# Which side of the on-chip memory the Fourier stage and the late weights lie on

## The chip, the cores and the metric

The kernel runs on one core of one Trainium2 chip, as one program. The metric is device time in microseconds (us) from start to end of the program. The times of the kernel before are 3048.86, 3058.79 and 3046.28 us (median 3048.86). "Within the measurement" below means within 0.5% of that, some 15 us.

## The reference, cut to what matters

The reference is one layer of an encoder over 1024 + 2048 tokens of width 1024, all in float32:

```python
u = rms_norm(h, norm_w)
z_f, u_f, z_s, xbc, dt_raw = split(u @ w_in)
four = fft2(u_f.reshape(b, s, 8, 64), axes=(1, 3), norm='ortho').real
y_f = einsum('bsgc,gcd->bsgd', four, w_fmix) * silu(z_f)
xbc = silu(conv1d_depthwise(xbc, conv_w) + conv_b)
y_s = ssd(xs, dt_f, A_f, B, C) + flip(ssd(flip(xs), ...)) + D * xs
y_s = group_rms_norm(y_s * silu(z_s)) * ssd_norm_w
h = h + concat([y_f, y_s]) @ w_out
h = h + (p @ w_ple_in) * sigmoid(h @ w_ple_gate)
y = rms_norm(h, final_norm_w)
```

## The kernel before, in words

The work has four stages, one after the other, with their edges overlapped.

**Stage 1, projections and SSD** (lines 102 to 821), three blocks of 1024 tokens. The normalized rows, turned and split into a high and a low part, lie in six tiles `uh0` to `uh2` and `ul0` to `ul2` of pool `up` (10,944 bytes in each partition). For each 128 columns of `w_in`, `piece` (line 340) makes 24 matmuls for each third of the tokens (L359). Around these pieces stands the SSD work of 12 units: `decays` loads 128 KB decay rows `er` (L633), `states` makes the states `H` (L605, L616), `diag` and `across` make `y` (L573, L647, L650, L651), `gated` multiplies by the gate on GpSimd (L656), `out` stores `y` (L665). The order of this stage is written out by hand, step by step. After the last piece some steps are left that hold only the end of the last unit: here "the tail". The pools of stage 1, from the left end of the memory to the right: `up` (normalized rows), `wp` (input weights: `wr`, `wh`, `wl`), `t4`, `cp` (conv rows and constants), `gp` and `sp` and `dp` (SSD tiles).

**Stage 2, Fourier** (lines 868 to 1033), eight steps: four of 1024 tokens, then four of 2048. Each loads `U` (L900) and the gate `Z` (L966), folds `U` (`Ue`, `Uo`, `fold0` to `fold3`: L969 to L979, on VectorE and GpSimd), multiplies by a small matrix (`pm` L959, `pq` L1004), splits the product (`qh` L1007, `ql` L1008) and multiplies by tables `th`, `tl` (L1013, `pr`). `yv` is put together on VectorE (L1023 to L1027), multiplied by `Z` on GpSimd (L1031) and stored (L1032). The tables come raw from DRAM into `traw` (L915) and are split (L916, L917). `th0` to `tl1` lie in pool `ft_`, `th2` to `tl3` in `fc`, what a step reads first in `fp`, the rest in `fq`.

**Stage 3, output product** (from line 1138), 24 pairs of 128-row tiles in 2 x 2 block products of Strassen's kind with weights `P1` to `P7`, each in a high tile `whP` and a low tile `wlP`. The raw weight is loaded into the low tile (L845), ScalarE copies it into the high tile (L847), VectorE leaves the rest in the low one (L848). `P1`, `P2`, `P6` lie in pool `wa` and are loaded during stage 2. `P5`, then `P7`, `P4`, `P3` lie in `wb` over tiles of stage 2; the loads of the second pair's `y` (L1158) are queued behind `P5`'s load (`issue_after`). The first pair is in `y_first` (pool `ox`). The other tiles are in `mp` and `yp`.

**Stage 4** is the gated second input and the last norm, with tiles of `mp` and `q4`.

Outside stage 1 a planner orders the instructions: it runs the program on a model of the engines, and each engine gets, when it is free in the model, the earliest instruction of the program that is ready. An instruction that writes a tile is ready once the tiles that held these bytes are done with (`reuse_waits="tile"`). The planner may also put instructions of stage 2 between the ones of stage 1 that were ordered by hand. On the chip each engine, SyncE's DMA queue among them, follows that order strictly.

A pool is placed on the left (the first goes lowest, next ones above) or on the right (the first goes highest, next ones below). Within a pool tiles ascend in the order in which they first appear. So it follows from the sizes what lies over what.

Of the kernel before, what the change touches and what calls it, by code (L numbers as in the profile page):

```python
# [9 lines left out]
F32 = mybir.dt.float32  # L10
# [5 lines left out]
PSUM = bass.MemoryType.PSUM  # L16
DRAM = bass.MemoryType.DRAM

P = 128
# [37 lines left out]
def tile_hybrid_encoder(ctx: ExitStack, tc: tile.TileContext, a):  # L57
# [767 lines left out]

    R_ = dict(side="right", reuse_waits="tile")
    L_ = dict(side="left", reuse_waits="tile")
    ox = ctx.enter_context(tc.tile_pool(name="ox", bufs=1, **L_))
    wa = ctx.enter_context(tc.tile_pool(name="wa", bufs=1, **L_))


    NAMES = ("P1", "P2", "P6", "P5", "P7", "P4", "P3")
# [6 lines left out]
    def product_weights(m, names, W):  # L839

        for name in names:
            pool = wa if name in NAMES[:3] else wb
            wh, wl = first_w.pop(name, None) or weight_tiles(pool, name)
            raw = wl.bitcast(F32)
            ld = nc.sync.dma_start(raw, WSd[m][:, NAMES.index(name)])  # L845
            for k in range(4):
                S.copy(wh[:, k, :], raw[:, k, :])  # L847
                V.tensor_tensor(wl[:, k, :], raw[:, k, :], wh[:, k, :].bitcast(F32), op=ALU.subtract)  # L848
            W[name] = (wh, wl)
        return ld  # L850

    def group_rstd(y, sq, sh, pb, rs):

        S.activation(sq, y.rearrange("p (r k) l -> p r k l", r=2)[:, :, 1:4, :], AF.Square)
        for j in (1, 2):
            G.tensor_tensor(sq[:, :, 0, :], sq[:, :, 0, :], sq[:, :, j, :], op=ALU.add)  # L856
        S.copy(sh[:, 0], sq[:, :, 0, :])
        G.tensor_tensor(sh[:, 1], sq[:, :, 0, :], sh[:, 0].bitcast(F32), op=ALU.subtract)
        for j in range(2):
            T.matmul(pb, lhsT=ones_r, rhs=sh[:, j], start=(j == 0), stop=(j == 1))  # L860
        S.activation(rs, pb, AF.Sqrt, bias=eps4, scale=1.0 / 384.0)
        V.reciprocal(rs, rs)

    def group_scale(y, rs):
        ssd = y.rearrange("p (r k) l -> p r k l", r=2)[:, :, 1:4, :]
        G.tensor_tensor(ssd, ssd, rs.unsqueeze(2).broadcast_to([P, 2, 3, P]), op=ALU.mult)

    with ExitStack() as ph:
        ft_ = ph.enter_context(tc.tile_pool(name="ft_", bufs=1, **R_))
        fp = ph.enter_context(tc.tile_pool(name="fp", bufs=2, **R_))  # L870
        fq = ph.enter_context(tc.tile_pool(name="fq", bufs=2, **L_))
        fc = ph.enter_context(tc.tile_pool(name="fc", bufs=1, **L_))
        fpr = ph.enter_context(tc.tile_pool(name="fpr", bufs=1, space=PSUM, **R_))
        fpl = ph.enter_context(tc.tile_pool(name="fpl", bufs=1, space=PSUM, **L_))
        shapes = dict(yv=([2048], 1, F32), Z=([2048], 1, F32), qh=([4, P], 2, F32R), ql=([4, P], 2, F32R),
                      ee=([512], 1, F32), eo=([512], 1, F32), ed=([2], 2, F32))

# [5 lines left out]
        def fq_next(tag):  # L883
            return fq_first.pop(tag) if tag in fq_first else fq_tile(tag)
# [47 lines left out]
        for step, (seq, f) in enumerate(order):  # L932
# [17 lines left out]
            def table(i, part, k):  # L950

                if N == 2048:
                    return tabs[i][part][:, k, :]
                return tabs[i % 2][part][:, k, i // 2:512:2]

            scale = 0.5 / math.sqrt(N * 64.0)
            pm = fpr.tile([P, 2, P], F32, tag="pm", name="pm")
            for i in range(2):
                T.matmul(pm[:, i, :], lhsT=bd[:, i, :], rhs=wbd[:, f, :], start=True, stop=True)  # L959
            mt = fp.tile([P, 2, P], F32, tag="mt", name="mt")  # L960
# [22 lines left out]
            S.activation(junk[:, 0:H + 1], Ue[:, 0:M + 1:2], AF.Copy, accum_out=edge[:, 1:2])  # L983
            S.activation(junk[:, 0:H], Ue[:, 1:M:2], AF.Copy, accum_out=edge[:, 2:3])
            V.tensor_tensor(edge[:, 1:2], edge[:, 1:2], edge[:, 2:3], op=ALU.subtract)
            pe = fpr.tile([P, 2], F32, tag="pm", name="pe")
            T.matmul(pe, lhsT=mats[0], rhs=edge[:, 0:2], start=True, stop=True)
            ed = fq_next("ed")
            V.tensor_copy(ed, pe)

            if last:
                for q in range(2):
                    pb = fpr.tile([P, 2, P], F32, tag="pm", name="pb")
                    sq = fp.tile([P, 2, 3, P], F32, tag="Uo", bufs=1, name="sq")
                    sh = fp.tile([P, 2, 2, P], F32R, tag="traw", name="sh")
                    rs = fp.tile([P, 2, P], F32, tag="fold0", name="rs")
                    group_rstd(y_first[:, q], sq, sh, pb, rs)
                    group_scale(y_first[:, q], rs)

            res = []  # L1000
            for i in range(4):
                pq = fpr.tile([P, 4, P], F32, tag="pq", bufs=2, name="pq")
                for k in range(kt):
                    T.matmul(pq[:, k, :], lhsT=folds[i][:, k * P:(k + 1) * P], rhs=mats[i % 2], start=True, stop=True)  # L1004
                qh = fq_next("qh")
                ql = fq_next("ql")
                S.copy(qh[:, :kt, :], pq[:, :kt, :])  # L1007
                V.tensor_tensor(ql[:, :kt, :], pq[:, :kt, :], qh[:, :kt, :].bitcast(F32), op=ALU.subtract)  # L1008
                pr = (fpr if i < 2 else fpl).tile([P, 512], F32, tag="pr", bufs=2 + i // 2, name="pr")
                n = 0  # L1010
                for k in range(kt):
                    for qt, part in ((qh, 0), (qh, 1), (ql, 0)):
                        T.matmul(pr[:, :H], lhsT=qt[:, k, :], rhs=table(i, part, k), start=(n == 0), stop=(n == 3 * kt - 1))  # L1013
                        n += 1
                res.append(pr)
# [13 lines left out]
            for q in range(N // TB):  # L1029
# [7 lines left out]

    wb = ctx.enter_context(tc.tile_pool(name="wb", bufs=1, **L_))  # L1040

    placed = {x: wb.tile([P, 4, 512], F32R, tag=f"w{x}", name=f"w{x}")
              for x in ("hP3", "hP4", "lP3", "lP4", "lP7", "lP5", "hP5", "hP7")}
    for name in NAMES[3:]:
        first_w[name] = placed["h" + name], placed["l" + name]
    mp = ctx.enter_context(tc.tile_pool(name="mp", bufs=1, **R_))
    mps = ctx.enter_context(tc.tile_pool(name="mps", bufs=1, space=PSUM, reuse_waits="tile"))
    todo = [(bi, c) for bi in range(3) for c in range(NCH)]
    NP = len(todo) // 2
# [58 lines left out]
    def turned(i):  # L1108

        hts, E = [], []  # L1110
        for bi, c in todo[2 * i:2 * i + 2]:
            hts.append(residual(Hd[bi * NCH + c]))

        def turn(src, nk):
            pt = mps.tile([P, 4, P], F32, tag="sm", bufs=3, name="pt")
            for k in range(nk):
                T.transpose(out=pt[:, k, :], in_=src[:, k * P:(k + 1) * P], identity=ident)
            return pt

        def kept21():  # L1120
            t = mp.tile([P, 4, P], F32, tag="s32", bufs=3, name="s32")
            S.copy(t, turn(hts[1], 4))
            return t
        A = halves(lambda: turn(hts[0], 4), lambda: turn(hts[0][:, 512:], 4), kept21, lambda: turn(hts[1][:, 512:], 4))
        for bi, c in todo[2 * i:2 * i + 2]:
            b = BLOCKS[bi]
            r0 = b["t0"] + c * P
            pl = q4.tile([P, 256], F32, tag="pl", bufs=2, name="pl")
            nc.sync.dma_start(pl, a["p"][b["seq"]][r0:r0 + P, :])
            pt = turn(pl, 2)  # L1130
            eh = q4.tile([P, 2, P], F32R, tag="eh", bufs=2, name="eh")
            el = q4.tile([P, 2, P], F32R, tag="el", bufs=2, name="el")
            S.copy(eh, pt[:, :2, :])
            V.tensor_tensor(el, pt[:, :2, :], eh.bitcast(F32), op=ALU.subtract)
            E.append((eh, el))
        return A, hts, E

    with ExitStack() as ph:
        yp = ph.enter_context(tc.tile_pool(name="yp", bufs=1, **R_))
        hbs, behind = [], []  # L1140

        def incoming(p):
            hb = yp.tile([P, 6, P], F32, tag="hb", name="hb")
            nc.sync.dma_start(hb, HBd[:, 6 * p:6 * p + 6, :])
            hbs.append(hb)
# [84 lines left out]
        for n, (p, i) in enumerate(steps):  # L1230
            cur, after = ready, coming
            with tc.issue_after(ld.ins):
                if n + 2 < len(steps):
                    if steps[n + 2] == (1, 0):
                        incoming(1)
                    coming = prepare(*steps[n + 2])
                if n + 1 < len(steps):
                    ready = after()
                else:
                    ph.close()  # L1240
                    q4 = ctx.enter_context(tc.tile_pool(name="q4", bufs=1, **R_))
                    ready = turned(0)
            outputs(i, W, *cur)
            if i == NP - 1:
                W = {}
                last_w = product_weights(p + 1, NAMES, W)
# [126 lines left out]
```

## Time and profile before

| | |
|---|---|
| median of three runs | 3048.86 us |
| profiled execution, its own time | 3053.19 us |
| its span, first to last instruction | 3051.3 us |
| TensorE busy (share of span) | 2837.5 us (93%) |
| TensorE weight loads | 2568.8 us (84%) |
| VectorE busy | 2238.1 us (73%) |
| ScalarE busy | 1387.5 us (45%) |
| GpSimd busy | 1477.0 us (48%) |
| mean granted TensorE clock | 0.973 |

Stage 1 ends near 1998 us, stage 2 near 2130 us, stage 3 near 2740 us. A busy share is a mean over stages with other limits; what a change of one seam is worth is read at that seam. Clock 1.00 is 2.4 GHz, 0.50 is 1.2 GHz.

### The profile page before, as it was taken

To read this page: it belongs to the slowest core of one execution; us is meant where nothing else is said; L and a number is where in the kernel's file an instruction comes from. 1 tells how busy PE (TensorE), PEld (TensorE's weight loads), DVE (VectorE), ACT (ScalarE), POOL (GpSimd) and SP (SyncE) were. 2 spreads that over 40 slices of the span, in tenths; PEclk is the share of its full clock that TensorE was granted. 3 is DMA by queue.
4 is the path that set the end of the run, shared out by engine and by line. 5 is a ranking of instruction groups with operands and counts; after the bars stand their busy time and mean duration, and the time that the engine had idled before them with its cause. 6 is when DMAs were issued, how large, how long until landed. Compare 5 with 4: busy or idle time off the path is not lost.

```text
span 3051.3 us, 47045 instructions
## 1 busy us (share of the span) xinstructions
PE 2837.5 (93%) x17252; PEld 2568.8 (84%) x17252; DVE 2238.1 (73%) x3412; ACT 1387.5 (45%) x2980; POOL 1477.0 (48%) x1114
## 2 busy tenths in 40 slices
PE   4999999999999989989999999969899989989998
PEld 4999988988999888978999999957677777768887
DVE  3687867766687667667679787677988988866665
ACT  3545455443544455433444444433434433355554
POOL 0355646441467566642555554455677688610000
PEclk9999999999999999999999999979999999999999
DMA  2378978872778678862677787665554644352221
GB/s 89 79 123 160 158 162 169 143 140 81 128 167 168 148 174 170 150 167 69 118 145 157 159 146 155 115 207 209 203 178 138 228 152 153 130 203 90 93 82 71
DMA packets 454579, 440.56 MB, mean 144 GB/s; under 512 B 24384, under 2 KB 405444, under 8 KB 450508
## 3 DMA queue, kind: packets, MB, share of 16 engines
q1 hardware_dynamic: 454060, 436.50, 59.8%
q8 instruction: 137, 2.24, 0.3%
q14 instruction: 94, 0.77, 0.1%
q10 hardware_dynamic: 288, 1.05, 0.1%
HBM read 328.41 MB, written 110.10 MB: 144 GB/s over the span
## 4 chain that ended last, share of the span: by engine, by line
PE 52%; DMA 15%; DVE 13%; POOL 9%; issue 6%; ACT 3%; SPq 2%; POOLq 0%; DVEq 0%; ACTq 0%
PE ps L359 27%; PE X L1089 6%; DMA wr<-in_w_in 4%; PE Z L1089 3%; DMA R<-ROWd 3%; PE pst L605 3%; DMA xt<-in_x_sample 2%; PE po L647 2%; PE W L1279 2%; DVE al L1060 2%; PE pd L573 2%; POOL wl L188 2%; DVE s L1065 2%; PE Y L1089 1%; POOL sq L856 1%
## 5 line engine op out<-in xcount | busy, mean ns | idle before, releaser
L359 PE MATMUL ps<-uh,wh 128*128 128x342 f32 (+1 forms) x2880 | 961.0, 334 | 5.2 <-ACT wh L187 5.2
L359 PE MATMUL ps<-uh,wl 128*128 128x342 f32 (+1 forms) x2880 | 927.7, 322 | 3.7 <-POOL wl L188 3.7
L359 PE MATMUL ps<-ul,wh 128*128 128x342 f32 (+1 forms) x2880 | 925.7, 321 | 0.0
L188 POOL TENSOR_TENSOR wl<-wr,wh 128x1024 fp32r<-128x1024 f32 x120 | 302.8, 2523 | 733.4 <-ACT wh L187 705.0
L359 PEld LDWEIGHTS ps<-uh,wh 128*128 128x128 f32 x2880 | 551.9, 192 | 16.4 <-ACT wh L187 5.7
L359 PEld LDWEIGHTS ps<-ul,wh 128*128 128x128 f32 x2880 | 554.2, 192 | 1.0 <-issue 1.0
L359 PEld LDWEIGHTS ps<-uh,wl 128*128 128x128 f32 x2880 | 550.5, 191 | 4.6 <-POOL wl L188 4.3
L556 ACT ACTIVATE R<-R,lb 128x128 f32<-128x128 f32 x1152 | 355.6, 391 | 69.7 <-POOL R L546 69.6
L546 POOL TENSOR_SCALAR_AFFINE_SELECT R<-R 128x512 f32<-128x512 f32 x288 | 260.3, 915 | 179.0 <-DMA R<-ROWd 168.7
L616 DVE SCALAR_TENSOR_TENSOR H<-H,cd,pst 128x64 f32<-128x64 f32 x888 | 182.7, 275 | 54.9 <-PE pst L605 51.9
L400 DVE SCALAR_TENSOR_TENSOR xT<-raw,cvt,xT 128x1024 f32<-128x1024 f32 x144 | 213.7, 1484 | 2.6
L365 ACT COPY raw<-ps 128x342 f32<-128x342 f32 x180 | 78.4, 439 | 279.2 <-PE ps L359 263.3
L1089 PE MATMUL X<-whP,ah 128*128 128x512 f32 x480 | 195.8, 408 | 8.4 <-ACT pu L1098 4.8
L585 POOL TENSOR_TENSOR xw<-xm,wd 128x512 f32<-128x512 f32 x144 | 181.0, 1261 | 33.2 <-PE pst L605 30.2
L1089 PE MATMUL X<-whP,al 128*128 128x512 f32 x480 | 193.0, 402 | 2.1 <-DVE al L1060 2.1
L1089 PE MATMUL X<-wlP,ah 128*128 128x512 f32 x480 | 193.7, 404 | 0.5 <-DVE wlP L848 0.5
L1201 POOL TENSOR_TENSOR ht<-ht,pu 128x512 f32<-128x512 f32 x96 | 155.8, 1631 | 62.2 <-ACT pu L1098 41.5
L605 PE MATMUL pst<-xw,Bm 128*128 128x128 f32 x1056 | 152.7, 287 | 24.8 <-POOL xw L585 24.7
L605 PEld LDWEIGHTS pst<-xw,Bm 128*128 128x128 f32 x1056 | 133.7, 194 | 41.2 <-POOL xw L585 29.4
L1060 DVE TENSOR_TENSOR al<-s,ah 128x512 fp32r<-128x512 f32 x144 | 141.5, 1005 | 20.0 <-ACT ah L1059 19.8
L187 ACT CAST wh<-wr 128x1024 fp32r<-128x1024 f32 x120 | 125.8, 1048 | 58.7 <-DMA wr<-in_w_in 58.5
L561 DVE TENSOR_TENSOR R<-R,R 128x512 f32<-128x512 f32 x144 | 141.3, 981 | 12.8 <-issue 6.3
(264 smaller groups left out, 5708.9 us busy)
## 6 DMA issues: line engine op xcount, KB each, us to landing
R<-ROWd SPq DMA_DIRECT2D x288, 256.0 KB
wr<-in_w_in SPq DMA_DIRECT2D x120, 512.0 KB
er<-EXPd SPq DMA_DIRECT2D x288, 128.0 KB
Hd<-ht SPq DMA_DIRECT2D x48, 512.0 KB
ht<-Hd SPq DMA_DIRECT2D x48, 512.0 KB
y<-Yd SPq DMA_DIRECT2D x46, 512.0 KB
wlP<-WSd SPq DMA_DIRECT2D x21, 1024.0 KB
Yd<-y SPq DMA_DIRECT2D x72, 256.0 KB
```

The lines of the kernel that those rows point to most:

```text
L188: G.tensor_tensor(wl, raw, wh.bitcast(F32), op=ALU.subtract)
L359: T.matmul(ps[:, :n], lhsT=wt[:, kt, :], rhs=ut[:, kt, :n], start=(i == 0), stop=(i == 3 * KT - 1))
L400: V.scalar_tensor_tensor(dst, raw[:, k:k + TB], cvt[:, 20 * k + ct:20 * k + ct + 1], dst, op0=ALU.mult, op1=ALU.add)
L546: G.affine_select(out=R.rearrange("p c h l -> p (c h) l"), in_=R.rearrange("p c h l -> p (c h) l"), pattern=[[0, 4], [sgn, P]], compare_op ...
L556: S.activation(R[:, c, h, :], R[:, c, h, :], AF.Exp, bias=self.B.lb[:, 2 * p + c, hc + h:hc + h + 1])
L561: V.tensor_tensor(E[0], E[0], E[1], op=ALU.add)
L585: G.tensor_tensor(xw, self.xm[c4].rearrange("p c (h e) -> p c h e", h=2), col(self.B.wd[:, c4:c4 + 4, hc:hc + 2]).broadcast_to([P, 4, 2, 6 ...
L605: T.matmul(pst[:, c, :], lhsT=B.Bm[self.g][:, c4 + c, :], rhs=xw[:, c, :, :].rearrange("p h e -> p (h e)"), start=True, stop=True)
L616: V.scalar_tensor_tensor(dst[:, e], H[d][:, cc, e], B.cd[:, cc, hc + h:hc + h + 1], pst[:, c, e], op0=ALU.mult, op1=ALU.add)
L1060: V.tensor_tensor(al, src, ah.bitcast(F32), op=ALU.subtract)
L1089: T.matmul(ps, lhsT=at[:, k, :], rhs=wt[:, k, :], start=(first and i == 0), stop=(i == 11), skip_group_check=not first)
L1201: return lambda t: G.tensor_tensor(h, h, t, op=ALU.add)
```

## The change

Nothing is computed otherwise, and no instruction is added or taken out. Pools change sides. `ft_` and `fp` go to the left, so they lie over `up` and `wp` and not over `gp`, `sp` and `dp`. `ox`, `wa`, `fc` and `fq` go to the right, in that order from the top. `wb` goes below `wa`, with its tiles in reverse order; `mp`, `yp` and `q4` go to the left. In PSUM the tiles `pm`, `pe`, `pb`, `pq` go to the left (three banks, those of the projections), and all five `pr` banks to the right.

```diff
-    ox = ctx.enter_context(tc.tile_pool(name="ox", bufs=1, **L_))
-    wa = ctx.enter_context(tc.tile_pool(name="wa", bufs=1, **L_))
+    ox = ctx.enter_context(tc.tile_pool(name="ox", bufs=1, **R_))
+    wa = ctx.enter_context(tc.tile_pool(name="wa", bufs=1, **R_))
...
-        ft_ = ph.enter_context(tc.tile_pool(name="ft_", bufs=1, **R_))
-        fp = ph.enter_context(tc.tile_pool(name="fp", bufs=2, **R_))
-        fq = ph.enter_context(tc.tile_pool(name="fq", bufs=2, **L_))
-        fc = ph.enter_context(tc.tile_pool(name="fc", bufs=1, **L_))
+        ft_ = ph.enter_context(tc.tile_pool(name="ft_", bufs=1, **L_))
+        fp = ph.enter_context(tc.tile_pool(name="fp", bufs=2, **L_))
+        fc = ph.enter_context(tc.tile_pool(name="fc", bufs=1, **R_))
+        fq = ph.enter_context(tc.tile_pool(name="fq", bufs=2, **R_))
+        fpl = ph.enter_context(tc.tile_pool(name="fpl", bufs=1, space=PSUM, **L_))
         fpr = ph.enter_context(tc.tile_pool(name="fpr", bufs=1, space=PSUM, **R_))
-        fpl = ph.enter_context(tc.tile_pool(name="fpl", bufs=1, space=PSUM, **L_))
...
-            pm = fpr.tile([P, 2, P], F32, tag="pm", name="pm")
+            pm = fpl.tile([P, 2, P], F32, tag="pm", name="pm")
...
-                pq = fpr.tile([P, 4, P], F32, tag="pq", bufs=2, name="pq")
+                pq = fpl.tile([P, 4, P], F32, tag="pq", bufs=2, name="pq")
...
-                pr = (fpr if i < 2 else fpl).tile([P, 512], F32, tag="pr", bufs=2 + i // 2, name="pr")
+                pr = fpr.tile([P, 512], F32, tag=f"pr{i // 2}", bufs=2 + i // 2, name="pr")
...
-    wb = ctx.enter_context(tc.tile_pool(name="wb", bufs=1, **L_))
+    wb = ctx.enter_context(tc.tile_pool(name="wb", bufs=1, **R_))
 
     placed = {x: wb.tile([P, 4, 512], F32R, tag=f"w{x}", name=f"w{x}")
-              for x in ("hP3", "hP4", "lP3", "lP4", "lP7", "lP5", "hP5", "hP7")}
+              for x in ("hP7", "hP5", "lP5", "lP7", "lP4", "lP3", "hP4", "hP3")}
...
-    mp = ctx.enter_context(tc.tile_pool(name="mp", bufs=1, **R_))
+    mp = ctx.enter_context(tc.tile_pool(name="mp", bufs=1, **L_))
...
-        yp = ph.enter_context(tc.tile_pool(name="yp", bufs=1, **R_))
+        yp = ph.enter_context(tc.tile_pool(name="yp", bufs=1, **L_))
...
-                    q4 = ctx.enter_context(tc.tile_pool(name="q4", bufs=1, **R_))
+                    q4 = ctx.enter_context(tc.tile_pool(name="q4", bufs=1, **L_))
```

## Rows read from the trace of the kernel before

**Rows 1.** Busy time by stretch: us, PE, PEld, DVE, ACT, POOL, clock, DMA share, GB/s.
```profile
1980.00:2000.00 20.00, 9.41 (x72) 8.06 (x70) 12.87 (x32) 2.79 (x9) 3.16 (x3) 0.79 0.53 145
2000.00:2020.00 20.00, 10.80 (x42) 9.49 (x42) 14.29 (x36) 6.89 (x22) 10.61 (x9) 0.50 0.73 223
...
2060.00:2080.00 20.00, 19.22 (x109) 16.49 (x109) 20.00 (x38) 12.02 (x25) 9.79 (x5) 1.00 0.80 293
...
2130.00:2170.00 40.00, 30.59 (x111) 20.47 (x109) 37.19 (x34) 18.41 (x36) 24.28 (x17) 0.96 0.74 260
```

**Rows 2.** TensorE in order of time: start, length, line, [idle before, its releaser].
```profile
1980.17 0.31 PE L359 MATMUL ps<-uh,wl 128*128 128x342 f32 x1
...
1984.91 1.11 PE L573 MATMUL pd<-R,xm 128*64 128x128 f32 x8 [2.08 <-DMA er<-EXPd]
...
1989.66 1.83 PE L647 MATMUL po<-CT,H 128*128 128x128 f32 x14
2006.34 1.19 PE L959 MATMUL pm<-wbd,bd 128*128 128x128 f32 x4 [14.85 <-DMA wbd<-in_w_fmix]
```

**Rows 3.** The chain that ended last, at the first seam: start, length, piece.
```profile
1980.47 14.88 DMA er<-EXPd
...
2000.39 5.36 DMA U<-UFd
```

**Rows 4.** SyncE's DMA queue in order of time at the first seam.
```profile
1977.14 7.15 SPq L633 DMA_DIRECT2D er<-EXPd  x4
1984.39 1.62 SPq L966 DMA_DIRECT2D Z<-ZFd  x1
...
1992.37 7.44 SPq L665 DMA_DIRECT2D Yd<-y  x2
...
2000.39 0.46 SPq L900 DMA_DIRECT2D U<-UFd  x1
```

**Rows 5.** VectorE in order of time, first seam and two folds later.
```profile
1990.92 0.74 DVE L578 SCALAR_TENSOR_TENSOR y<-xT,dsk,pd 128x512 f32<-128x512 f32 x1
1995.47 0.56 DVE L650 TENSOR_TENSOR yt<-po,er 128x384 f32<-128x384 f32 x1 [3.81 <-DMA er<-EXPd]
...
1997.44 0.69 DVE L651 TENSOR_TENSOR y<-y,yt 128x512 f32<-128x512 f32 x1
...
2005.77 0.69 DVE L969 TENSOR_TENSOR Ue<-U 128x511 f32<-128x511 f32 x1 [4.10 <-DMA U<-UFd]
...
2032.95 2.27 DVE L974 TENSOR_TENSOR fold<-Ue 128x512 f32<-128x512 f32 x1
...
2073.99 0.68 DVE L974 TENSOR_TENSOR fold<-Ue 128x512 f32<-128x512 f32 x1
```

**Rows 6.** Short stretches around the falls of the clock, columns as in the first group.
```profile
1986.00:1988.00 2.00, 2.00 (x10) 2.00 (x10) 1.48 (x3) 0.00 (x0) 0.00 (x0) 0.50 0.66 165
...
2022.00:2024.00 2.00, 2.00 (x11) 2.00 (x10) 1.02 (x4) 1.88 (x7) 0.00 (x0) 0.50 0.61 133
```

**Rows 7.** SyncE's DMA queue at the second seam.
```profile
2129.22 0.33 SPq L845 DMA_DIRECT2D wlP<-WSd  x1
2129.64 1.01 SPq L1158 DMA_DIRECT2D y<-Yd  x2
...
2146.88 1.00 SPq L1158 DMA_DIRECT2D y<-Yd  x2
```

**Rows 8.** GpSimd in order of time there: the last two gate products.
```profile
2130.12 5.21 POOL L1031 TENSOR_TENSOR yv<-yv,Z 128x1024 f32<-128x1024 f32 x2 [7.70 <-DVE yv L1026]
```

**Rows 9.** ScalarE and its DMA queue in order of time there.
```profile
2137.77 0.33 ACTq L1032 DMA_DIRECT2D Yd<-yv  x1
...
2138.71 2.18 ACT L847 CAST whP<-wlP 128x512 fp32r<-128x512 f32 x4
```

**Rows 10.** What SyncE's queue waited for, 2110 to 2180: us in total, times, longest.
```profile
SPq L1158 <- DMA Yd<-yv: 7.5, 1, 7.5
```

**Rows 11.** VectorE by line, 2130 to 2170: instructions, busy us, mean ns, idle before.
```profile
L848 DVE TENSOR_TENSOR wlP<-wlP,whP 128x512 fp32r<-128x512 f32 x16 | 18.6, 1224 | 0.0
```

More of the change, by code (lines that the diff above doesn't have):

```diff
@@ L985, in tile_hybrid_encoder @@
             V.tensor_tensor(edge[:, 1:2], edge[:, 1:2], edge[:, 2:3], op=ALU.subtract)
-            pe = fpr.tile([P, 2], F32, tag="pm", name="pe")
+            pe = fpl.tile([P, 2], F32, tag="pm", name="pe")
             T.matmul(pe, lhsT=mats[0], rhs=edge[:, 0:2], start=True, stop=True)
@@ L992, in tile_hybrid_encoder @@
                 for q in range(2):
-                    pb = fpr.tile([P, 2, P], F32, tag="pm", name="pb")
+                    pb = fpl.tile([P, 2, P], F32, tag="pm", name="pb")
                     sq = fp.tile([P, 2, 3, P], F32, tag="Uo", bufs=1, name="sq")
```

## The prediction

> **What bounds the kernel now.** I read first the page's slices: TensorE is busy 8 or 9 tenths in all of them but the first and the 27th (1983 to 2060 us), where stage 1 passes into the Fourier stage. Then I read busy time by stretch there and at the next seam, where the Fourier stage passes into the output product [rows 1]. From 1980 to 2000 TensorE works 9.41 of 20 us, from 2000 to 2020 10.80, and those at 0.50, the 1.2 GHz level. VectorE starts its Fourier work at 2005.77 (below) and is busy 14.29 us up to 2020, that is all of the time, 20.00 of 20 from 2060, and 37.19 of 40 in 2130 to 2170: behind both seams VectorE is the limit, not TensorE.
>
> TensorE's own order [rows 2] shows the first hole. The last projection starts at 1980.17, the last tail work ends at 1991.5, and the next matmul stands at 2006.34 after 14.85 us, released by the load of `wbd`. The chain of waits [rows 3] goes through `er`, 14.88 us, and then through the load of `U`, 5.36 us. Between the two lies SyncE's queue [rows 4]: two `Yd` stores hold it from 1992.37 for 7.44 us, since they wait for the gated `y`; `U` is issued at 2000.39 behind them. One load of the Fourier stage did go earlier: `Z` at 1984.39, ahead of stores that precede it in the program. `Z` lies on the left, over `wr` and `wh`; `U`, `bd`, `wbd` and `traw` lie on the right, over `CT`, `zT`, `xT`, `Bm`, the last of which are read until the tail's end.
>
> VectorE [rows 5] has finished a run of tail work at 1990.92 + 0.74 = 1991.66, waits 3.81 us for `er`, ends the tail at 1997.44 + 0.69 = 1998.13, and starts the first `Ue` at 2005.77, after 4.10 us of waiting for `U`.
>
> **The change part by part.** No instruction comes or goes; only what a slot waits for.
>
> *First seam.* From the sizes: `ft_` (32,768 bytes a partition) and `fp` (some 51,400) now begin where `up` begins. `up` and `wp` together take 86,144, so both pools lie wholly over normalized rows and input weights, all done with when the last projection ends, about 1980.5 (`U`'s first buffer reaches into `uh2`, so not before). `pm` and `pq` stand in the projections' banks. So the Fourier inputs need nothing of the tail. What then comes last?
>
> (a) The loads. `U` can take the place that `Z` has in the queue, 1984.39 and some issues on: behind eight `er` loads, ahead of the `Yd` stores. How soon does it land? Nearest rows: `U` itself, 5.36 us on a quiet queue, and `er`, 14.88 us in just this stretch [rows 3]. From an issue between 1984.4 and 1987 that gives 1989.8 to 2001.9; I take the middle, 1995.
>
> (b) VectorE. Its queue is strict. The planner gives the tail precedence where the tail is ready in its model, and in the kernel before it put the stage's first memsets behind the last `y`, as if its model saw nothing of the 3.81 us wait for `er`. So I expect `Ue` behind the tail, at 1998.1 (the memsets, with slots free early now, go ahead). This is later than (a). Gain 2005.77 - 1998.13 = 7.6 us. Ends: with `U` only at 2001.9, 3.9; with `Ue` filling the wait at 1991.66, and the four tail operations (2 x 0.56 + 2 x 0.69 = 2.5) paid behind, 2005.77 - 1991.66 - 2.5 = 11.6.
>
> Behind that VectorE is the limit [rows 1], so the shift goes through. The later table loads, `wa` and `y_first` are issued by their place in the stage, from its fifth step on, and move with it; their new slots, over `gp`, `sp`, `dp`, are free when the tail ends. If one of them did hold its step, the wait could be no longer than the shift itself.
>
> A faster clock I cost at nothing: TensorE waits 2.08 us before 1984.91 [rows 2] and in 1986 to 1988 the clock is at 0.50, the 1.2 GHz level [rows 6], so a hole of some 7 us instead of 14.85 will lower it too. Its price is small as long as VectorE is the limit: in 2022 to 2024, still at 0.50, VectorE idles 0.98 of 2 us [rows 6]; two such stretches, 2 us, are the other end.
>
> The GpSimd folds can now run beside VectorE's tail. A fold on VectorE takes 0.68 alone and 2.27 beside GpSimd work [rows 5]. The Trainium skill ("SBUF — State Buffer", Who interferes with whom) says that a VectorE operation with two SBUF inputs and a GpSimd one that reads SBUF lock each other out for a whole instruction; that agrees with these two rows, and speaks against the early start. By it one or two of the tail's operations would stand 1.6 us longer each and the gain be 4.4 to 6.0; it is inside the ends above.
>
> *Second seam.* Here the new order is no mirror: `fc` and `fq` have changed places too. `P5`'s low tile lay over `th3`, `tl2`; now it lies over `Z` and `qh`. Its high tile and `P7`'s lie over `yv`. `P4` and `P3`, needed last, now lie over the tables. Before, `P5`'s load was issued at 2129.22 [rows 7], when the tables were read for the last time. Now it waits for the last product with `Z`, which ends at 2130.12 + 5.21 = 2135.33 [rows 8]: 6.1 us later, and the second pair's `y` (2129.64) is queued behind it. The copy into the high tile, at 2138.71, must further wait for the last `yv` store, issued on ScalarE's queue at 2137.77 [rows 9]; SyncE's queue was released by such a store at 2146.88, after 7.5 us [rows 7, 10]. So the copy comes 0 to 8.2 us later. Queued behind it on ScalarE are the copies of the other weights and of the second pair, and VectorE's splits wait for them. But `P4` and `P3` can now be loaded ahead of `P5`, when the tables are read, and their eight splits can come first: sixteen splits take 18.6 us [rows 11] of the 37.19 that VectorE works in 40 [rows 1], so eight, 9.3, would fill a wait of 8.2. The planner orders by readiness, and `A22` times `P4` has a bank of its own. The gain end is an estimate: a third of the 9.4 us that TensorE stands idle in these 40 [rows 1], 3. I take a loss of 1 us, between -3 and 8.2, near the cover.
>
> *The rest* (`mp`, `yp`, `q4` on the left, `ox`, the PSUM banks of stage 3) I cost at nothing: `ah`, `al`, `s32` now lie over `th1`, `tl1`, `bd`, `U`, which the last step has read two table products before its end. The planner can order the remaining 900 us otherwise, since its model starts from other times; no row bounds this, and the range has 2 to 3 us for it either way.
>
> Sum: -7.6 + 1 = -6.6 us. On the profiled execution's 3053.19 (span 3051.3, and 1.9 around it that the change leaves alone) that is 3046.6; that execution is 4.3 over the median of the runs, 3048.86, so for a median I say 3042.3.
>
> **The rivals.**
>
> A. *The ring.* `U` lands behind everything issued before it. For it: `er` took 14.88 us from issue to its reader, with DMA engines busy only half [rows 1, 3]. Against: `Z` and stores ran in the same stretch. `Ue` at about 2002, gain 3.9, less 1: 3046. The Trainium skill ("DMA: Bandwidth & Descriptors", Queues, rings and completion order) says that each DMA engine takes descriptors in ring order, which would give this case; no row here shows it per engine.
>
> B. *It does not do what it says.* The planner leaves the loads behind the `Yd` stores, as before. For it: `bd`, `U` and the others stood there [rows 4]. Against: `Z` did not, and it was the only one whose slot was free. Gain 0, second seam 1: 3049 to 3050.
>
> C. *Slower.* `P5` is the price: the planner's model lands the `yv` store early, puts `P5`'s copies and splits at their old place in ScalarE's and VectorE's strict queues, and these stand until the store has landed, with `P7`, `P4`, `P3` behind. +8.2, against a first seam at its low end, 3.9: +4.3, 3053. It decides once the second seam loses more than the first gains, so from 3.9 on at the low end, from 7.6 at my value. For it: `P5` is needed first and gets the latest slots. Against: VectorE's work can be drawn forward.
>
> D. *More than I say.* `Ue` fills the wait (11.6) and the early `P4` and `P3` give 3: -14.6, 3034.
>
> **How the numbers follow.** Forecast 0.50 (its own range 3037 to 3047), A 0.13, B 0.09, C 0.13, D 0.15. The range 3031 to 3053 takes in C and most of D, and some of the later order; what it leaves out holds 2 in 10 with the noise of the runs. Faster by over 0.5% (15.2 us, about what a measurement can tell from no change) needs D and a little: 0.15. Slower by as much needs C and a bad order later: 0.04. Within: 0.81.
>
> **What would show it.** Right: `U` issued before the last `Yd` stores, at 1984 to 1988; `Ue` directly behind the last `y` on VectorE, near 1998; TensorE's hole near 7 us; `P5`'s load released by GpSimd's product with `Z`, and `P4`'s load ahead of it. Wrong: `U` still behind the stores (B), `Ue` waiting for its load past 2000 (A), `Ue` between tail operations (D), ScalarE standing before `P5`'s copy for some 8 us with VectorE idle (C). A time below 3031 would mean that a bound other than VectorE set the first seam.

## The result, and the profile after

The changed kernel takes 3060.02 us (median of 12 runs, 3056.74 to 3068.84) beside 3048.69 us for the kernel before on the same chip (12 runs, 3037.99 to 3058.79): ratio 1.0042, 95% interval 1.0029 to 1.0055. It is slower by some 11 us where 6.6 us less were forecast, and it lies outside the range given.

The profiled execution of after took 3068.84 us, span 3067.1. Part of its distance to the profiled execution of before is neither kernel's: stage 1, in the same order in both, ends its projections at 1980.49 in the one and at 1986.37 in the other, and between 1967 and 1974 in the other profiled executions below. So the stretches here are counted from the end of the last projection or from a later event.

**First seam.** VectorE of the changed kernel in order of time (start, length, line, what; idle before and its releaser in brackets):

```profile
1987.99 1.23 DVE L616 SCALAR_TENSOR_TENSOR H<-H,cd,pst 128x64 f32<-128x64 f32 x6
1989.14 0.68 DVE L561 TENSOR_TENSOR R<-R,R 128x512 f32<-128x512 f32 x1
2003.68 0.69 DVE L969 TENSOR_TENSOR Ue<-U 128x511 f32<-128x511 f32 x1 [13.86 <-DMA U<-UFd]
2004.41 1.63 DVE L562 TENSOR_TENSOR R<-R,cb 128x512 f32<-128x512 f32 x1
...
2026.07 0.68 DVE L651 TENSOR_TENSOR y<-y,yt 128x512 f32<-128x512 f32 x1
```

Against [rows 5]: the first `Ue` now stands between two tail operations, the addition and the product that make one `R`, and waits 13.86 us for `U`. The rest of the tail waits behind it and is then worked off between Fourier operations; its last `y` ends at 2026.75, 40.4 us after the projections instead of 17.6. In the first 20 us after the projections VectorE is busy for 5.61 us, in the kernel before for 12.87. TensorE and SyncE's queue there:

```profile
1986.06 0.31 PE L359 MATMUL ps<-uh,wl 128*128 128x342 f32 x1
...
2006.30 1.12 PE L573 MATMUL pd<-R,xm 128*64 128x128 f32 x8 [17.58 <-DVE H L616]
2010.16 3.75 PE L647 MATMUL po<-CT,H 128*128 128x128 f32 x16 [1.58 <-DVE H L616]
2023.39 1.22 PE L959 MATMUL pm<-wbd,bd 128*128 128x128 f32 x4 [5.71 <-DVE ed L989]
```
```profile
1982.23 0.70 SPq L286 DMA_DIRECT2D UFd<-ft  x1
1982.97 8.13 SPq L633 DMA_DIRECT2D er<-EXPd  x4
1991.14 1.14 SPq L887 DMA_DIRECT2D bd<-in_bdft  x1
1992.38 2.63 SPq L900 DMA_DIRECT2D U<-UFd  x1
```

The hole of 14.85 us [rows 2] is now 17.58 us long and stands ahead of tail matmuls instead of behind them. `U` did move: it is issued 6.0 us after the projections' end (1992.38 - 1986.37), ahead of the `Yd` stores, where it stood 19.9 us after it [rows 2, 4]. Next to nothing came of that: from the end of the projections to the end of the last product with a table it is 148.7 us before and 148.2 after.

**Second seam.** ScalarE with its DMA queue, then SyncE's queue, of the changed kernel:

```profile
2142.44 0.62 ACT L1059 CAST ah<-s 128x512 fp32r<-128x512 f32 x1 [7.25 <-DVE s L1065]
2142.50 0.33 ACTq L1032 DMA_DIRECT2D Yd<-yv  x1
2142.96 0.58 ACT L1098 COPY pu<-X 128x512 f32<-128x512 f32 x1
2148.25 0.59 ACT L1098 COPY pu<-X 128x512 f32<-128x512 f32 x1 [4.70 <-PE X L1089]
2149.71 2.18 ACT L847 CAST whP<-wlP 128x512 fp32r<-128x512 f32 x4 [0.88 <-DMA Yd<-yv]
```
```profile
2140.68 0.33 SPq L845 DMA_DIRECT2D wlP<-WSd  x1
2141.06 1.05 SPq L1158 DMA_DIRECT2D y<-Yd  x2
2142.22 4.99 SPq L845 DMA_DIRECT2D wlP<-WSd  x3
```

The last table product ends at 2134.60 (2129.19 before). `P5`'s load is issued 6.1 us after it and not at once [rows 7]; its copy into the high tile starts 15.1 us after it and not 9.5 [rows 9]. There are two reasons in these rows. The copy waits for the landing of the last `yv` store, 0.88 us. But ahead of it stands the second `pu`, which waited 4.70 us for TensorE, and TensorE had waited for the first `pu`, which is queued behind the copy of `S4` (`ah<-s`, 2142.44) and that behind VectorE. In the kernel before the first `pu` is ahead of it:

```profile
2132.93 0.59 ACT L1098 COPY pu<-X 128x512 f32<-128x512 f32 x1 [2.36 <-POOL yv L1031]
2137.71 0.62 ACT L1059 CAST ah<-s 128x512 fp32r<-128x512 f32 x1 [4.19 <-DVE s L1065]
```

In the 20 us behind the last table product VectorE's busy time falls from 17.74 to 11.56 us (third number), by the rows of before and after for that stretch, columns as in [rows 1]. Its first splits of `P5` wait 6.04 us for ScalarE's copy:

```profile
2129.19:2149.19 20.00, 16.05 (x58) 11.39 (x58) 17.74 (x18) 10.54 (x21) 11.80 (x9) 0.91 0.96 351
2134.60:2154.60 20.00, 14.14 (x46) 10.40 (x46) 11.56 (x12) 5.46 (x11) 7.99 (x5) 0.83 0.73 262
```
```profile
2150.42 2.50 DVE L848 TENSOR_TENSOR wlP<-wlP,whP 128x512 fp32r<-128x512 f32 x4 [6.04 <-ACT whP L847]
```

From the last table product to the fifth store of products (L1220) it is 92.85 us instead of 87.11: 5.7 us lost.

### The profile page after: what moved, and what is told of

It is laid out like the page before. It is cut to its first block, busy times and chain, and to the rows that moved or that the text cites. A ratio compares the mean times of both kernels' runs of the same rounds, so it can differ in the third digit from the quotient of the medians.

```text
span 3067.1 us, 47029 instructions
## 1 busy us (share of the span) xinstructions
PE 2837.6 (93%) x17252; PEld 2569.4 (84%) x17252; DVE 2231.5 (73%) x3412; ACT 1389.4 (45%) x2980; POOL 1455.6 (47%) x1114
## 4 chain that ended last, share of the span: by engine, by line
PE 55%; DMA 14%; DVE 13%; POOL 8%; issue 5%; ACT 3%; SPq 2%; POOLq 0%; DVEq 0%; ACTq 0%
PE ps L359 29%; DMA wr<-in_w_in 6%; PE X L1089 6%; PE Z L1089 3%; PE pst L605 3%; PE po L647 2%; DMA xt<-in_x_sample 2%; PE W L1279 2%; DVE al L1060 2%; DMA R<-ROWd 2%; PE pd L573 2%; POOL wl L188 2%; DVE s L1065 2%; PE Y L1089 1%; PE pr L1013 1%
## 5 line engine op out<-in xcount | busy, mean ns | idle before, releaser
L546 POOL TENSOR_SCALAR_AFFINE_SELECT R<-R 128x512 f32<-128x512 f32 x288 | 252.2, 887 | 192.2 <-DMA R<-ROWd 184.9
L1060 DVE TENSOR_TENSOR al<-s,ah 128x512 fp32r<-128x512 f32 x144 | 143.8, 1020 | 17.9 <-ACT ah L1059 17.6
```

Of the source, the lines that this page charges most:

```text
L546: G.affine_select(out=R.rearrange("p c h l -> p (c h) l"), in_=R.rearrange("p c h l -> p (c h) l"), pattern=[[0, 4], [sgn, P]], compare_op ...
L1060: V.tensor_tensor(al, src, ah.bitcast(F32), op=ALU.subtract)
```

## The experiments

Each was profiled, and all but the last two were timed (12 runs, mirror 6) beside the kernel before on the same chip. The table gives, from one profiled execution each, four stretches in us: A from the end of the last projection to the end of the last table product, B from there to the issue of the fifth store of products (L1220), C to the 25th of the 48 stores, D to the issue of the first output (L1300); and the timed ratio to before. Some expectations call these two stores the ninth and the last, and count D only to where SyncE begins to wait for the first output, 4 to 8 us earlier.

How far one profile can be trusted shows where kernels share a seam. In stretch A pulate has the order of before (148.7 and 147.0), and pufirst and again have that of after (148.2, 147.6, 148.1); in B hold and again have the seam of after (92.9, 92.2, 93.1). So a difference below 2 us in A, or 1 us in B, says little.

| kernel | A | B | C | D | ratio, 95% interval |
|---|---|---|---|---|---|
| before | 148.7 | 87.1 | 241.0 | 296.0 | 1 |
| after | 148.2 | 92.9 | 242.6 | 298.8 | 1.0042, 1.0029 to 1.0055 |
| mirror | 155.0 | 91.3 | 240.9 | 292.9 | 1.0049, 1.0033 to 1.0065 |
| hold | 140.5 | 92.2 | 241.9 | 292.0 | 1.0007, 0.9992 to 1.0022 |
| both | 139.9 | 92.3 | 242.0 | 296.6 | 1.0023, 1.0010 to 1.0037 |
| bswap | 144.5 | 90.1 | 239.7 | 294.1 | 0.9997, 0.9983 to 1.0011 |
| pulate | 147.0 | 91.9 | 240.8 | 296.5 | 1.0013, 0.9999 to 1.0027 |
| pufirst | 147.6 | 93.2 | 240.5 | 295.7 | 1.0025, 1.0011 to 1.0039 |
| mirror_pu | 154.8 | 86.4 | 241.6 | 289.3 | 1.0023, 1.0010 to 1.0036 |
| all | 138.2 | 87.0 | 240.8 | 293.4 | 0.9979, 0.9966 to 0.9992 |
| noer | 140.9 | 94.7 | 241.9 | 293.8 | not timed |
| again (= after) | 148.1 | 93.1 | 243.0 | 294.2 | not timed |

**mirror**: P5 and P7 over the tables again.

```
-        fc = ph.enter_context(tc.tile_pool(name="fc", bufs=1, **R_))
         fq = ph.enter_context(tc.tile_pool(name="fq", bufs=2, **R_))
+        fc = ph.enter_context(tc.tile_pool(name="fc", bufs=1, **R_))
```

> The changed kernel with fq and fc declared the other way round, so that P5 and P7 lie over the tables again and P3, P4 over yv and Z. Theory 1 (P5's slot is what the second seam costs): P5's load is released when the tables are read for the last time, its first copy stands within 2 to 3 us of the last product with a table instead of 15.1 us (2149.71 - 2134.60), the second seam gives back about 5.6 us: 3054.4; if the 4.8 us that the changed kernel loses later, between 2345 and 2745 us, hang on P5 as well, 3049.6. Theory 2 (the place of P5 is innocent, another order made by the planner costs the time): no gain, 3060 +- 2, with the loss between last table product and first product store as before. The first seam stays as it is under both: VectorE's first Ue between tail operations.

`P5`'s load is released at once, 2122.34 against a last table product at 2122.27. Its copy starts at 2136.23 all the same, 14.0 us after it, behind the second `pu`:

```profile
2130.10 0.62 ACT L1059 CAST ah<-s 128x512 fp32r<-128x512 f32 x1 [7.20 <-DVE s L1065]
2130.62 0.58 ACT L1098 COPY pu<-X 128x512 f32<-128x512 f32 x1
2135.75 0.58 ACT L1098 COPY pu<-X 128x512 f32<-128x512 f32 x1 [4.55 <-PE X L1089]
2136.23 2.18 ACT L847 CAST whP<-wlP 128x512 fp32r<-128x512 f32 x4
```

Theory 1 in its simple form, that `P5`'s slot is the cause, falls: B gives back 1.6 us and the ratio nothing. This kernel also loses 7 us more in stretch A, as mirror_pu does and both does not; the Fourier steps are interleaved in another order in it, and what in that order costs the 7 us was not followed up.

**hold**: VectorE's and TensorE's Fourier work behind the tail (`tail` keeps the last tail instruction of each engine).

```
-        first_u = [load_u(0, 0)]
+        first_u = [load_u(0, 0)]; [ph.enter_context(tc.issue_after(tail[e].ins)) for e in "VT"]
```

> The changed kernel with VectorE's and TensorE's Fourier work ordered behind the last tail operation of each. Theory 1 (the first seam gave nothing because Ue stands ahead of the tail in VectorE's strict queue and holds it until U has landed): the tail ends within about 6 us of 1998, TensorE's hole of 17.58 us before the last pd goes to under 5 us, Ue starts at 2004 to 2006, the first table product at about 2014 instead of 2026, and the time falls by 6 to 8 us: 3053. Theory 2 (the late landing of U alone sets the seam; the tail is short and fits anywhere): Ue starts where it did, the tail's few us are only moved from behind it to before it, 3058 to 3060. The second seam is not touched.

Stretch A falls by 7.7 us against after, and the ratio by 3.5 parts in 1000, some 10.7 us. VectorE and GpSimd:

```profile
1991.38 0.69 DVE L651 TENSOR_TENSOR y<-y,yt 128x512 f32<-128x512 f32 x1
1995.16 3.34 DVE L917 TENSOR_TENSOR tl<-traw,th 128x512 fp32r<-128x512 f32 x2 [3.08 <-ACT th L916]
1998.42 0.68 DVE L969 TENSOR_TENSOR Ue<-U 128x511 f32<-128x511 f32 x1
```
```profile
1992.30 1.27 POOL L970 TENSOR_TENSOR Uo<-U 128x511 f32<-128x511 f32 x1 [16.21 <-DMA U<-UFd]
```

The tail ends 17.7 us after the projections, `U` has landed by 1992.30, 17.9 us after them, and `Ue` follows with two table splits in between. Theory 1 holds: with the tail ahead, VectorE is busy for 12.37 us of the first 20 instead of 5.61, and the first table product starts 28.2 us after the projections instead of 40.0. `Ue` itself stands later than in after, 24.0 us after the projections instead of 17.3, and only 1.3 us sooner than in before (25.3). Against before, what comes sooner is the work around it: the first `Uo` on GpSimd at 17.9 us and not 25.4, `pm` on TensorE at 19.7 and not 25.9, the first table product at 28.2 and not 32.1. So these 7.7 us, or 8.2 against before, are not the forecast's 7.6, which came from an earlier `Ue`.

**both**: the two edits together.

> The two edits together: Fourier work behind the tail, and P5, P7 over the tables. Theory 1 for both seams: 3060 - 7 - 5.6 = 3047.4, and 3042.6 if the later 4.8 us go with P5's place. If either theory 2 holds, the time of the other run alone: 3053 or 3054.4; if both do, 3060.

Stretch A is that of hold; stretch B does not move, 92.3. No theory had a time above hold's. In the profiles its D is 4.6 us longer than hold's; why was not followed up.

**bswap**: the kernel before with `fc` and `fq` exchanged on the left.

```
-        fq = ph.enter_context(tc.tile_pool(name="fq", bufs=2, **L_))
         fc = ph.enter_context(tc.tile_pool(name="fc", bufs=1, **L_))
+        fq = ph.enter_context(tc.tile_pool(name="fq", bufs=2, **L_))
```

> The kernel before with fq and fc declared the other way round on the left, and nothing else: P5 and P7 lie over yv, Z, qh and P3, P4 over the tables, as in the changed kernel, while the first seam stays that of before. Theory 1: the loss of the second seam shows alone, 3048.7 + 5.6 = 3054.3, and 3059 if the later 4.8 us hang on it. Theory 2 (place of P5 innocent): 3048.7 +- 2.

The instructions of all five engines stand in the same order as in before, but for one `Z` load in SyncE's queue. `P5`'s copy waits 1.76 us for its load and starts 11.4 us after the last table product; B is 3.0 us longer.

```profile
2124.55 2.18 ACT L847 CAST whP<-wlP 128x512 fp32r<-128x512 f32 x4 [1.76 <-DMA wlP<-WSd]
```

The timed ratio shows nothing of it, 0.9997. In the profiled execution A is 4.2 us shorter: with that `Z` load two places later VectorE waits 0.95 and 0.81 us for `er` instead of 3.81 [rows 5]. So the slot seems to have a price, but 3 and not 5.6 us, and that on stretch B of one profile.

**pulate**: before, with one pair of ScalarE's instructions exchanged (`s4` holds the copy of the first `S4`).

```
-            p1 = kept(X)
+            with (tc.issue_after(s4.pop().ins) if s4 else ExitStack()): p1 = kept(X)
```

> The kernel before with one pair of ScalarE's instructions exchanged: at the second seam the copy of the first product (pu) stands behind the copy of S4, as it does in the changed kernel; no slot is touched, and VectorE's and TensorE's orders are those of before. Theory 3 (ScalarE's order is one of two overlapping causes): pu waits for S4, some 4.7 us later; TensorE stands some 3.4 us before S2 times P6; the second pu and P5's copy, queued behind it, move from 9.5 to about 14 us after the last table product; time + 4 us, ratio to before 1.0014. Theory 1 (P5's slot alone): nothing changes, 1.000.

ScalarE's and TensorE's rows are those expected:

```profile
2125.23 0.58 ACT L1098 COPY pu<-X 128x512 f32<-128x512 f32 x1
2130.31 0.59 ACT L1098 COPY pu<-X 128x512 f32<-128x512 f32 x1 [4.50 <-PE X L1089]
2130.79 2.18 ACT L847 CAST whP<-wlP 128x512 fp32r<-128x512 f32 x4
```
```profile
2125.86 0.80 PE L1089 MATMUL X<-whP,ah 128*128 128x512 f32 x1 [4.09 <-ACT pu L1098]
```

With the last table product at 2116.19, `P5`'s copy is 14.6 us after it, B is 4.8 us longer, and the ratio is 1.0013 where the theory had 1.0014, though its interval just holds 1. The order of two copies alone does most of what the second seam lost, with no slot changed.

**pufirst**: after, with the pair exchanged back. The first product and its copy are traced ahead of `S4`'s copy:

```
+        X = bank("X"); product(X, A, W, "A11", "P1"); p1 = kept(X)
+        early.append((X, p1)); return tc.issue_after(copied[0].ins)
...
-        two("S4", diff(a12, s2, ALU.subtract))
+        with (ExitStack() if "P5" in W else first_product(A)): two("S4", diff(a12, s2, ALU.subtract))
```

> The changed kernel with the same pair exchanged back (pu ahead of S4's copy), all slots as changed. Theory 3: TensorE's hole of 3.39 us before S2 times P6 goes, but P5's copy still stands until the last yv store has landed, about 15 us after the last table product; the time falls by 1 us at most, 3059 to 3060, ratio to before 1.004. If the order alone were the cause: P5's copy 9.5 to 11 us after the last table product, 4 us less, 3056, ratio 1.003.

The hole before `S2` times `P6` is gone, and `P5`'s copy now stands for the other cause, 16.2 us after the last table product (2117.87):

```profile
2126.31 0.59 ACT L1098 COPY pu<-X 128x512 f32<-128x512 f32 x1
2134.11 2.18 ACT L847 CAST whP<-wlP 128x512 fp32r<-128x512 f32 x4 [7.21 <-DMA Yd<-yv]
```

B stays at 93.2. The ratio came out lower than expected, 1.0025 and not 1.004. Its interval overlaps that of after, and in the profile C is 2.1 us shorter; at the seam nothing is gained.

**mirror_pu**: slot and order both put back.

> Both at the second seam: pu ahead of S4's copy and P5, P7 over the tables. Theory 3: P5's copy 9.5 us after the last table product as in the kernel before, and the stretch from the last table product to the ninth product store 87 us instead of 91 to 93; ratio to before 1.0049 (that of the run mirror) less 4 us, 1.0036. If neither is the cause, the stretch stays at 91 us and the ratio at 1.0049.

B is 86.4, that of before. `P5`'s copy:

```profile
2130.31 0.58 ACT L1098 COPY pu<-X 128x512 f32<-128x512 f32 x1
2130.79 2.18 ACT L847 CAST whP<-wlP 128x512 fp32r<-128x512 f32 x4
```

The last table product was at 2121.88, so it starts 8.9 us after it. Theory 3 holds: slot and order each hide the other. One alone costs 3.0 (bswap) or 4.8 us (pulate), both together 5.1 to 6 (hold, after, again), and taking one away gives back at most 1.6 (mirror; nothing in both) or nothing (pufirst). The ratio, 1.0023, is lower than the 1.0036 expected, which lies at the end of its interval; A keeps mirror's 155.

**all**: hold, mirror and pufirst, and the first table splits on VectorE behind the first folds.

```
+            with tc.issue_after(V.tensor_tensor(folds[2][:, :H], Ue[:, 0:H], Ue[:, M:H:-1], op=ALU.subtract).ins): [run(f) for f in late]; late.clear()
```

> Every edit together: Fourier work behind the tail on VectorE and TensorE, the first table splits on VectorE behind the first folds (in the run hold they stood ahead of Ue, which waited with them until 1998.42 though U had landed by 1992.30 and the tail had ended at 1992.07), P5 and P7 over the tables, pu ahead of S4's copy. Theory: from hold's 1.0007, 4 to 6 us less at the first seam and 4 to 5 us less at the second: ratio 0.997 to 0.998, some 3034 to 3037 where the kernel before takes 3042.8. If the seams do not add up: no better than hold, 1.0007.

3034.48 us (12 runs, 3027.36 to 3044.56) beside 3041.16 for before on the same chip. It is faster than the kernel before by 0.2%, and its interval does not hold 1. `Ue` now follows the tail directly; A is 138.2 and B 87.0, so the seams add up:

```profile
1985.86 0.69 DVE L651 TENSOR_TENSOR y<-y,yt 128x512 f32<-128x512 f32 x1
1986.64 0.69 DVE L969 TENSOR_TENSOR Ue<-U 128x511 f32<-128x511 f32 x1
```

Here, and not in hold, `Ue` stands where the forecast had it: 18.0 us after the projections, 7.3 sooner than in before, with A 10.5 us shorter than before. Of the 4 to 6 us expected against hold from the earlier `Ue`, A shows 2: the matmul that makes `pm` still waits for its load until 1988.51, and ScalarE's copy of the first table until 1988.99.

**noer**: after, without the last four `er` loads.

```
+                if self.B.bi == 2 and self.u == NU - 1 and c4 == 4:
+                    self.er[d, 4] = self.er[d, 0]
+                    return
```

> The changed kernel without the last four er loads of stage 1 (the last unit's second half takes the decays of its first half; that part of the output is left wrong). Ring theory: U, issued behind fewer er loads, lands some 6 us after its issue, as the 5.36 us of the kernel before, instead of 11.3 us, and Ue starts some 8 to 13 us after the last projection's end instead of 17.3. Rival (U waits for its own store and load; er is beside the point): still 10 to 11 us from issue to landing, Ue moved by no more than the issue itself moves.

SyncE's queue and the first reader of `U` that does nothing else meanwhile (three lines further down in this kernel's text):

```profile
1969.77 0.69 SPq L286 DMA_DIRECT2D UFd<-ft  x1
1970.50 3.27 SPq L890 DMA_DIRECT2D bd<-in_bdft  x1
1973.94 2.29 SPq L903 DMA_DIRECT2D U<-UFd  x1
```
```profile
1984.19 1.70 POOL L973 TENSOR_TENSOR Uo<-U 128x511 f32<-128x511 f32 x1 [10.54 <-DMA U<-UFd]
```

From issue to landing it is still 10.25 us, so the ring theory falls as it was put. What the `er` loads cost `U` is their issue: 8.13 us of SyncE in after, 6.55 in again. Without them `Ue` starts 10.2 us after the projections instead of 17.3 and A is 7 us shorter.

**again**: the changed kernel profiled once more.

> The changed kernel itself, profiled a second time. If the later losses belong to the change: the stretch from the ninth to the last product store again 242.6 us (241.0 before) and from there to the first output 290.5 us (287.8 before). If they are one execution's: 240.5 to 241.5 and 285.5 to 288.5, as in the other runs. The second seam, from the last table product to the ninth product store, must stay at 92 to 93 us, and the first seam's order as it was.

C is 243.0, near the 242.6 of the first profile; D is 294.2 and not 298.8. So some 2 us in C seem to belong to the kernel, and the 2.8 us in D to one execution. A and B repeat within 0.3 us.

## Why the prediction was wrong, point by point

**Loads ahead of the `Yd` stores, `U` in `Z`'s place.** Right. Issue was forecast at 3.9 to 6.5 us after the projections' end (1984.4 to 1987 less 1980.5) and came at 6.0. Rival B is out. Rival A's `Ue`, some 21 us after the projections, did not come either, and noer speaks against its mechanism.

**(a) `U`'s landing.** Inside its ends. 1995 is 14.5 us after the projections, with ends at 9.3 and 21.4; it landed after 17.3, and after 17.2 in again. In the clock of before that is 1997.8, still ahead of the tail's end at 1998.1.

**(b) VectorE.** This is the first step that failed: "So I expect `Ue` behind the tail, at 1998.1". The planner put it ahead of all but the start of the tail. I had read from [rows 5] that the planner's model sees nothing of the wait for `er`, and concluded that it gives the tail precedence. A model that lands `er` early lands `U` early too, and then `Ue` is ready while VectorE has nothing else; I used the blindness on one side only. That reason is argued. That the order is the cause is shown by hold, which changes only the order and brings 7.7 us. That this is close to the forecast 7.6 is luck: in hold `Ue` gains 1.3 us on before, and in all, where it gains 7.3 by the forecast's own order, A is 10.5 us shorter, so the gain is not the shift of `Ue` alone. Rival D had `Ue` early as well, but as a gain, with the tail paid behind it; it did not ask what stands behind `Ue` if `U` is late.

**Clock, GpSimd's folds.** Costed at nothing, or left inside the ends; no run took these apart.

**Second seam.** The second step that failed: "I take a loss of 1 us". It measured 5.7. The cover that I named, `P4` and `P3` loaded and split ahead of `P5`, was not used: SyncE issues `P5` first and the other three at 2142.22, and VectorE waits 6.04 us before the first split. What I had priced, the wait for the slot, is 3.0 us alone (bswap), inside the ends of -3 to 8.2. What none of the cases had is the exchange of the first `pu` and `S4`'s copy, 4.8 us alone (pulate), although the text says that the order can change. Why VectorE is late with `S4` stands in the trace of both kernels: in before three `al` take 5.98 us and in after two take 5.36 while GpSimd's two products with `Z` run (5.21 [rows 8] and 5.20), and one just behind them takes 0.68:

```profile
2130.50 5.98 DVE L1060 TENSOR_TENSOR al<-s,ah 128x512 fp32r<-128x512 f32 x3
```
```profile
2135.46 5.20 POOL L1031 TENSOR_TENSOR yv<-yv,Z 128x1024 f32<-128x1024 f32 x2 [8.98 <-DVE yv L1026]
```
```profile
2135.84 5.36 DVE L1060 TENSOR_TENSOR al<-s,ah 128x512 fp32r<-128x512 f32 x2
2141.12 0.68 DVE L1060 TENSOR_TENSOR al<-y_first,ah 128x512 fp32r<-128x512 f32 x1
```

`S4`'s copy starts 8.5 us after the last table product in before and 7.8 in after, so VectorE's delay is common to both; only ScalarE's order makes the first `pu` pay for it.

The Trainium skill ("SBUF — State Buffer", Who interferes with whom) says that a VectorE operation with two inputs in SBUF and a GpSimd one that reads SBUF lock each other out for a whole instruction; these rows agree.

**The rest at nothing.** C costs some 2 us, within the 2 to 3 us that the range held for it; what costs them was not followed up.

**The sum.** Forecast -7.6 + 1 = -6.6; measured about 0 (hold: 7.7 possible) + 5.7 + 2, some 8 where the times differ by 11 (9 to 17 by the interval). The rest is not located: from the last projection to its end the profiled execution of after is 9.9 us longer than that of before, and again 5.8. Rival C had the place and the copy that waits, and 3053, but with a gain of 3.9 at the first seam that did not come.

## What to carry to other kernels

Where a planner orders the work, a slot that comes free earlier also makes its reader ready earlier in the planner's model; before counting the gain, ask what stands behind that reader in its engine's strict queue if the load lands late. Two waits that end close together hide each other: an experiment that removes one may show next to nothing, so remove each alone and both together, on the kernel before as well as on the one after. And when executions differ by up to 19 us over a stage that is the same in all, before the changed part even begins, count stretches from an event just ahead of the change.

## What the runs showed that was not expected

From its issue to the first `Uo` `U` takes 10.3 to 11.9 us in all nine kernels and executions that issue it 4 to 11 us after the store of the data that it reads, with `er` loads between the two or without (noer). Issued 21 to 24 us after that store it takes 4.6 us (bswap, pulate) or 5.5 (before). The store itself can take longer than that: in hold the chain of waits goes through it, from there to the next store and a table load:

```profile
1970.27 15.65 DMA UFd<-ft
```

So an early issue buys less than its distance. That `U` is slow because of the store is not shown; what sets the 10 us and more was not tried.
